# One run of all eight units in place of two of four, in the transposes' four banks, with the blocks reordered

## The chip, the cores and the metric

The kernel runs on one core of one Trainium2 chip. The metric is the device time of one execution in microseconds; lower is better. Engines are named as in the profile: PE is TensorE, DVE is VectorE, ACT is ScalarE, POOL is GpSimd, SP is SyncE, and PEld is the weight load of PE.

## What is computed

One decoder layer on 256 tokens of width 4096: a norm, one wide input projection, two groups that work on its columns, and one output projection.

```python
proj = einsum('btd,dc->btc', rms_norm(x, norm_pre_g), w_in)       # 4096 -> 14528 columns
rwkv_in, g_rwkv, glu_v, glu_g, g_conv = split(proj)
xs = rwkv_in + (prev - rwkv_in) * mu_shift                          # r, k, v and two bottlenecks
S_t = S_{t-1} diag(w_t) + (S_{t-1} (-kk_t)) (kk_t a_t)^T + v_t k_t^T # 32 heads of 64
y_t = S_t r_t
y_rwkv = (group_norm(y) * lnx_g + lnx_b + bonus) * silu(g_rwkv)
c = depthwise_conv31(glu_v * sigmoid(glu_g)) + conv_b
c = silu(layer_norm(c)) @ w_pw2 + b_pw2
y_conv = c * silu(g_conv)
out = concat(y_rwkv, y_conv) @ w_out
return x + rms_norm(out, norm_post_g)
```

## The kernel before

**The main product.** The three projections are 41 blocks of up to 512 output columns: 29 for `w_in`, 4 for `w_pw2`, 8 for `w_out`. A block is a row of slots, one for each 128 rows of its weights (32, 16 and 32). In a slot the weight tile is split into a rounded half `wh` (ACT, `w_hi`) and the rest `wl` (DVE, `w_lo`), and PE runs six matmuls, three for each half of the tokens, into `acc`. `w_hi` is issued 4 slots ahead and `w_lo` 3 (`HI_LEAD`, `LO_LEAD`).

**The side work.** What the two groups need is written as generators (`job_shift`, `job_prep`, `job_inv`, `job_chain`, `job_conv`, `job_ln`, `job_gate` and others) in lanes "0" to "5". The order on PE, DVE and ACT is written out by the program: behind each slot's matmuls `Side.step` calls the lanes in their order, one step of each, and goes on with those that yielded 0, as long as `room` holds, that is, while the summed costs of DVE and of ACT lie below those of PE. The costs are the program's own formulas (`dve_cost`, `act_cost`, `pe_cost`); a small matmul counts 45 ns, a main one of 512 columns 0.417 x 512 + 3. `CREDIT` limits how far an idle engine's sum may lag. Where the main product needs something that the side work has not issued yet (`side.drain`), the lanes run on without main matmuls.

**The recurrence.** 32 heads are 8 units of 4. For each unit `job_prep` builds records of 8 chunks of 32 tokens and stores them in `rec_dr`; for each two units `job_inv` inverts the small triangular matrices (`t_x`, loaded back as `c_x`). `job_chain` then walks through the 8 chunks for four units at a time, so it runs twice. `side_of` splits the four units of a run into two sides that use opposite rows of the array. In a chunk PE has three groups of small matmuls into `pz`, two banks wide: G12, the records' product (`qs` by `uv`) and the state's product (`ar` by `S`); G3, the inverse (`xt` by `ry`); G45, the growth of the state (`bkt` by `uv`) and the outputs (`qs` by `uv`). In G12 the units of side 1 are done in two halves of 32 columns (`HALVES`). Between the groups ACT copies `ry`, ACT and DVE copy `uv`, and DVE adds the outputs and the state. The yields between them put each at least one slot behind the last. The third and fourth `job_inv` wait for the first run's end. PSUM's eight banks are 4 for `acc`, 2 for transposes and other short products (`tp`), 2 for `pz`.

**The order of blocks.** For each group g of two units: k, r, v, then the gate and value blocks of the convolution (`gg`, `gv`); then `gc` (4), `g` (4), `w_pw2` (4), `w_out` (8). A block's eviction into one of two `pt` tiles adds its jobs. `job_conv` transposes `gv` and runs 31 taps on DVE in lane 5, the last in order. `job_ln` starts when the recurrence and the four convolutions are done, and the first block of `w_pw2` needs its result, four of its 16 rows at a time.

## Time and profile before

| | |
|---|---|
| median of 3 runs | 1817.35 us (1817.13 to 1818.72) |
| the profiled execution | 1820.06 us, span 1818.3 us |
| PE busy | 1805.0 us |
| PEld busy | 1486.4 us |
| DVE busy | 1339.7 us |
| ACT busy | 1011.6 us |
| POOL busy | 204.7 us |
| moved by DMA | 404.93 MB |

Busy time is the union of an engine's instructions. An engine's mean over the span hides stages in which it is full. A matmul's duration overlaps the next one's, so what a matmul costs PE is read from the distance of starts. An fp32 matmul that is no transpose shows as two records.

### The profile page before, as it was taken

The numbers are of one execution on the slowest core, as the hardware profiler recorded it, in microseconds if no ns is written. First come the engines' busy times: TensorE is split into PE (matmuls) and PEld (weight loads), VectorE is DVE, ScalarE is ACT, GpSimd is POOL, SyncE is SP. The second block draws the span as 40 slices with busy tenths as digits, with TensorE's granted clock in tenths as the row PEclk, the third lists the DMA queues.
The fourth block names the chain that finished last, engine by engine and source line by source line (L and its number), as shares of the span: only waits on it lengthen the run. The fifth ranks groups of instructions, "written<-read, shape, count | busy, mean of one in ns | idle before, by whom it ended". The sixth has DMA issues, their size and how long they took to land.

```text
span 1818.3 us, 30793 instructions
## 1 busy us (share of the span) xinstructions
PE 1805.0 (99%) x11152; PEld 1486.4 (82%) x11152; DVE 1339.7 (74%) x2668; ACT 1011.6 (56%) x1753; POOL 204.7 (11%) x346
## 2 busy tenths in 40 slices
PE   9999999999999999999999999999999999999997
PEld 7899888888878877788888888778888888888886
DVE  6655778997789976799998898567766655555555
ACT  6756665556645564555566544445575444554453
POOL 0000112031120302021041212010100000000000
PEclk9999999999999999999999999999999999999999
DMA  9867678777787778678677878766877666666665
GB/s 323 276 177 197 206 213 250 202 203 215 214 240 203 203 231 260 207 222 252 189 224 226 253 219 255 235 219 200 290 228 258 237 196 198 200 193 203 200 200 189
DMA packets 205144, 404.93 MB, mean 223 GB/s; under 512 B 16448, under 2 KB 33984, under 8 KB 204736
## 3 DMA queue, kind: packets, MB, share of 16 engines
q1 hardware_dynamic: 182224, 335.18, 60.7%
q0 software_dynamic: 22624, 67.66, 11.9%
q8 instruction: 87, 1.43, 0.3%
q14 instruction: 65, 0.53, 0.1%
q10 hardware_dynamic: 144, 0.13, 0.0%
HBM read 371.45 MB, written 31.46 MB: 222 GB/s over the span
## 4 chain that ended last, share of the span: by engine, by line
PE 97%; DVE 1%; DMA 1%; issue 0%; ACT 0%; POOL 0%; DVEq 0%; POOLq 0%
PE acc L92 91%; PE tp L92 3%; PE pz L92 2%; DMA c_y<-n_dr 1%; DVE chl L92 0%; DVE wl L92 0%; DVE cw L92 0%; DMA c_ar<-in_xT 0%; DVE c_y L92 0%; POOL c_y L624 0%; ACT wh L92 0%; DVE c_st L92 0%; ACT c_st L92 0%; DVE t_bk L92 0%; DVE c_s L92 0%
## 5 line engine op out<-in xcount | busy, mean ns | idle before, releaser
L92 ACT ACTIVATE wh<-wr 128x512 fp32r<-128x512 f32 (+1 forms) x1243 | 767.0, 623 | 652.6 <-PE acc L92 381.2
L92 DVE TENSOR_TENSOR wl<-wr,wh 128x512 fp32r<-128x512 f32 (+1 forms) x1243 | 830.5, 677 | 328.8 <-ACT wh L92 321.6
L92 PE MATMUL acc<-wh,lh 128*128 128x512 f32 (+1 forms) x2358 | 923.9, 392 | 1.2 <-ACT wh L92 1.2
L92 PE MATMUL acc<-wl,lh 128*128 128x512 f32 (+1 forms) x2358 | 911.8, 387 | 0.8 <-DVE wl L92 0.8
L92 PE MATMUL acc<-wh,ll 128*128 128x512 f32 (+1 forms) x2358 | 911.5, 387 | 0.0
L92 PEld LDWEIGHTS acc<-wh,lh 128*128 128x128 f32 x2358 | 443.3, 188 | 90.5 <-ACT wh L92 2.5
L92 PEld LDWEIGHTS acc<-wh,ll 128*128 128x128 f32 x2358 | 443.1, 188 | 88.6
L92 PEld LDWEIGHTS acc<-wl,lh 128*128 128x128 f32 x2358 | 443.7, 188 | 86.1 <-DVE wl L92 3.0
L92 DVE SCALAR_TENSOR_TENSOR cw<-up,pv,cw 128x256 f32<-128x256 f32 x480 | 218.0, 477 | 0.4
L92 PE MATMUL acc<-wh,chl 128*128 128x512 f32 x256 | 82.4, 397 | 0.0
L92 PEld LDWEIGHTS acc<-wh,chl 128*128 128x128 f32 x256 | 48.2, 188 | 10.9
L92 PE MATMUL acc<-wl,chl 128*128 128x512 f32 x128 | 50.5, 394 | 0.0
L533 POOL DMA_DIRECT2D rec_dr<-c_ar x16 | 14.4, 903 | 279.6 <-DVE c_ar L92 270.3
L92 ACT ACT_TABLE_LOAD x32 | 41.1, 1283 | 3.1 <-PE tp L92 1.4
L92 DVE TENSOR_SCALAR c_st<-pz 32x256 f32<-32x256 f32 x32 | 13.6, 426 | 33.8 <-ACT c_st L92 33.4
L1079 POOL DMA_DIRECT2D bb<-in_norm_post_g x8 | 4.3, 539 | 303.3 <-DVE chl L92 258.8
L649 POOL DMA_DIRECT2D c_x<-x_dr x64 | 35.1, 555 | 17.5 <-DMA x_dr<-t_x 15.3
L680 POOL DMA_DIRECT2D c_st<-rec_dr x32 | 17.1, 538 | 159.1 <-DVE c_st L92 83.9
L92 DVE TENSOR_TENSOR c_sq<-t_x,c_y 128x120 f32<-128x120 f32 (+24 forms) x124 | 31.6, 255 | 4.5 <-DMA c_y<-n_dr 4.5
L92 ACT ACTIVATE pt<-acc,rstd 128x512 f32<-128x512 f32 (+3 forms) x52 | 33.9, 656 | 0.6
L92 PEld LDWEIGHTS pz<-c_st 32*32 32x32 f32 (+2 forms) x1728 | 22.3, 116 | 13.4 <-PE acc L92 4.6
L92 DVE TENSOR_TENSOR t_x<-t_x,c_sq 128x120 f32<-128x120 f32 (+24 forms) x124 | 31.5, 254 | 0.0
(184 smaller groups left out, 945.8 us busy)
## 6 DMA issues: line engine op xcount, KB each, us to landing
wr<-in_w_in SPq DMA_DIRECT2D x430, 512.0 KB, 4.5
wr<-in_w_out SPq DMA_DIRECT2D x128, 512.0 KB, 4.6
c_st<-rec_dr POOLq DMA_DIRECT2D x32, 512.0 KB, 6.9
wr<-in_w_pw SPq DMA_DIRECT2D x32, 512.0 KB, 4.4
wr<-in_w_in SPq DMA_DIRECT2D x16, 352.0 KB, 3.3
rec_dr<-c_ar POOLq DMA_DIRECT2D x16, 256.0 KB, 5.6
rec_dr<-c_q POOLq DMA_DIRECT2D x16, 256.0 KB, 4.5
rec_dr<-c_bkt POOLq DMA_DIRECT2D x8, 512.0 KB, 5.3
```

The source lines that it names most:

```text
L92: return f(*args, **kw)
L533: nc.gpsimd.dma_start(out=rec_dr[qd, :, :, un, 0, q * 64:q * 64 + 64].rearrange("c p x -> p c x"), in_=ar[:, q * 8:q * 8 + 8, :])
L649: nc.gpsimd.dma_start(out=xt[y * CH:(y + 1) * CH, un, h * 4:h * 4 + 4], in_=x_dr[2 * pr + un, y ^ (2 * h), h * 4:h * 4 + 4].rearrange("g i ...
L680: nc.gpsimd.dma_start(out=recs[c][:, un].rearrange("p n i h x -> p (n i h x)"), in_=rec_dr[qd, c, :, un].rearrange("p n i x -> p (n i x)"))
L1079: nc.gpsimd.dma_start(out=gb, in_=a["norm_post_g"][0:1, j * BN:(j + 1) * BN].broadcast_to([P, BN]))
```

## The change

`side_of` now puts units 0 to 3 on one side and 4 to 7 on the other, and `job_chain` runs once, over all eight units. `pz` is four banks wide and is opened in the four banks that transposes use otherwise (`open_mid`, `TP` = 4 in place of 2); while it is open, `tp_wait` lets no transpose start. The first products of G12 alternate between the sides and have no halves, as G3 and the outputs do. The chain opens its own SBUF pool where the preparations' was, and three more yields stand between its steps; records come in four parts instead of two, the same number of DMAs in all. The third and fourth inversion no longer wait for the first run. The blocks go k, r, v of all groups first, with only the first convolution's among them; those of the second and third convolution follow, then three `gc` blocks, the fourth convolution's and the last `gc`. `job_conv` is split: `job_up` transposes in lane 1, the taps stay in lane 5, with 8 `up` buffers for 3. In the closing normalisation the squares of one slice overlap the subtraction of the next.

```diff
+TP = 4
...
+    mid = {}
+
+    def open_mid(name, bufs):
+        if mid:
+            mid["ctx"].close()
+        mid["ctx"] = ctx.enter_context(ExitStack())
+        mid["pool"] = mid["ctx"].enter_context(tc.tile_pool(name=name, bufs=bufs, space=PSUM))
+
+    open_mid("ps_tp", TP)
...
     def tp_wait():
-        while tpn[0] >= 2:
+        while tpn[0] >= TP or "run" in rw:
...
     def side_of(u):
-        return u // 2 % 2
+        return u // 4
...
-        while ("n", 2 * pr + 1) not in rw or (pr > 1 and not rw.get(("done", pr // 2 - 1))):
+        while ("n", 2 * pr + 1) not in rw:
...
-    def job_chain(qd):
-
-        rp = rw["pool"]
-        while ("prepd", 4 * qd + 3) not in rw or "xt" not in rw["quad", qd]:
+        rw["inv", pr] = True
+
+    def job_chain():
+
+        while any(("prepd", u) not in rw for u in range(8)) or any(("inv", pr) not in rw for pr in range(4)):
             yield "wait"
-        d = rw.pop(("quad", qd))
-        pc, xt = d["pc"], d["xt"]
-        ys = rp.tile([P, 4, 4, 2, 64], F32, name="c_y", bufs=1)
-        S = pz = ry = None
+        rw["run"] = True
+        while tpn[0] > 0:
+            yield "wait"
+        for _ in range(3):
+            yield
+        rw["ctx"].close()
+        rw["ctx"] = ExitStack()
+        rp = rw["pool"] = rw["ctx"].enter_context(tc.tile_pool(name="rc", bufs=1))
+        open_mid("ps_ch", 1)
+        pc, xt = rw["pc"], rw["xt"]
+        ys = rp.tile([P, 4, 8, 2, 64], F32, name="c_y", bufs=1)
+        S = ry = None
+
+        pz = mid["pool"].tile([P, 4, 4, P], F32, name="pz")
 
         RX, RD = slice(0, 64), slice(64, 128)
-        UN = range(4)
-        SIDES = ((0, slice(0, 2)), (1, slice(2, 4)))
-        PAIRS = (0, 2, 1, 3)
-        HALVES = ((slice(0, 64),), (slice(0, 32), slice(32, 64)))
+        UN = range(8)
+        PAIRS = (0, 4, 1, 5, 2, 6, 3, 7)
         recs = {}
 
-        def fetch(c, half):
+        def fetch(c, part):
 
             if c < NCH:
-                if half == 0:
-                    recs[c] = rp.tile([P, 4, 4, 2, 64], F32, name="c_st", bufs=2)
-                un = slice(2 * half, 2 * half + 2)
-                hold(recs[c][:, 2 * half, 0, 0, 0:1])
-                nc.gpsimd.dma_start(out=recs[c][:, un].rearrange("p n i h x -> p (n i h x)"), in_=rec_dr[qd, c, :, un].rearrange("p n i x -> p (n i x)"))
+                if part == 0:
+                    recs[c] = rp.tile([P, 8, 4, 2, 64], F32, name="c_st", bufs=2)
+                un = slice(2 * part, 2 * part + 2)
+                hold(recs[c][:, 2 * part, 0, 0, 0:1])
+                nc.gpsimd.dma_start(out=recs[c][:, un].rearrange("p n i h x -> p (n i h x)"), in_=rec_dr[c, :, un].rearrange("p n i x -> p (n i x)"))
 
         def swap(x):
             return x.rearrange("p b n x -> p n b x")
 
         def outputs(c):
-            if c % 2 == 0:
-                vec.tensor_tensor(out=ys[:, c // 2], in0=swap(pz[:, :, :, RX]), in1=ry, op=ALU.add)
-            else:
-                for sd, nn in SIDES:
-                    for rows in VR[1 - sd]:
-                        vec.tensor_tensor(out=ys[rows, c // 2, nn], in0=swap(pz[rows, :, nn, RX]), in1=ry[rows, nn], op=ALU.add)
-
-        for _ in range(8):
-            yield
-        for half in range(2):
-            fetch(0, half)
-            yield
+            for sd in range(2):
+                b = slice(2 * sd, 2 * sd + 2)
+                for rows in VR[1 - sd] if c % 2 else (slice(0, P),):
+                    vec.tensor_tensor(out=swap(ys[rows, c // 2, 4 * sd:4 * sd + 4]), in0=pz[rows, b, :, RX], in1=ry[rows, b], op=ALU.add)
+
+        for part in range(4):
+            fetch(0, part)
             yield
         for _ in range(5):
             yield
         for c in range(NCH):
-            vrs, urs = ([R[(c + n // 2) % 2] for n in UN] for R in (VR, UR))
+            vrs, urs = ([R[(c + u // 4) % 2] for u in UN] for R in (VR, UR))
             ar, qs, bkt, uv = (recs[c][:, :, i] for i in range(4))
             if c > 0:
                 outputs(c - 1)
-                Sn = rp.tile([P, 4, 2, 64], F32, name="c_s", bufs=2)
-                dec = pc[:, :, c - 1::8].unsqueeze(3).broadcast_to([P, 4, 2, 64])
+                yield
+                Sn = rp.tile([P, 16, 64], F32, name="c_s", bufs=2)
+                dec = pc.rearrange("p s q n c -> p (s q n) c")[:, :, c - 1:c].broadcast_to([P, 16, 64])
+                grown = pz[:, :, :, RD].rearrange("p b n x -> p (b n) x")
                 if S is None:
-                    vec.tensor_tensor(out=Sn, in0=swap(pz[:, :, :, RD]), in1=dec, op=ALU.mult)
+                    vec.tensor_tensor(out=Sn, in0=grown, in1=dec, op=ALU.mult)
                 else:
-                    vec.tensor_tensor(out=Sn, in0=swap(pz[:, :, :, RD]), in1=S, op=ALU.add)
+                    vec.tensor_tensor(out=Sn, in0=grown, in1=S, op=ALU.add)
                     vec.tensor_tensor(out=Sn, in0=Sn, in1=dec, op=ALU.mult)
                 S = Sn
                 yield
-                fetch(c + 1, 0)
                 yield
-                fetch(c + 1, 1)
-            else:
-                fetch(1, 0)
-            pz = ps_ch.tile([P, 2, 4, P], F32, name="pz")
-
-            for n in UN:
-
-                for o in HALVES[n // 2]:
-                    for q, h in DIAG:
-                        pe.matmul(pz[HS[q ^ h], h, n, RX][o], qs[vrs[n][q], n, h, o], uv[vrs[n][q], n, h, :], start=n == 0, stop=S is None and n == 3)
-            for n in UN if S is not None else ():
+            fetch(c + 1, 0)
+            yield
+            fetch(c + 1, 1)
+            for u in PAIRS:
                 for q, h in DIAG:
-                    pe.matmul(pz[HS[q ^ h], h, n, RX], ar[HS[h], n, q, :], S[HS[h], n, q, :], start=False, stop=n == 3)
-            if c == 0:
-                fetch(1, 1)
-            yield
-            ry = rp.tile([P, 4, 2, 64], F32, name="t_x", bufs=1)
-            act(out=ry, in_=swap(pz[:, :, :, RX]), func=AF.Copy)
-            yield
-            for n in PAIRS:
-                ur = urs[n]
+                    pe.matmul(pz[HS[q ^ h], u // 4 * 2 + h, u % 4, RX], qs[vrs[u][q], u, h, :], uv[vrs[u][q], u, h, :],
+                              start=u % 4 == 0, stop=S is None and u % 4 == 3)
+            for u in UN if S is not None else ():
                 for q, h in DIAG:
-                    pe.matmul(pz[ur[q], h, n, RX], xt[ur[q ^ h], n, h * 4 + c // 2, :], ry[ur[q ^ h], n, h, :], start=True, stop=True)
-            yield
-            for sd, nn in SIDES:
-                ur = urs[2 * sd]
-                act(out=uv[ur[0], nn], in_=swap(pz[ur[0], :, nn, RX]), func=AF.Copy, scale=-1.0)
-                vec.tensor_scalar(out=uv[ur[1], nn], in0=swap(pz[ur[1], :, nn, RX]), scalar1=-1.0, scalar2=None, op0=ALU.mult)
-            yield
-            for n in UN if c < NCH - 1 else ():
+                    pe.matmul(pz[HS[q ^ h], u // 4 * 2 + h, u % 4, RX], ar[HS[h], u, q, :], S[HS[h], u // 4 * 8 + q * 4 + u % 4, :],
+                              start=False, stop=u % 4 == 3)
+            yield
+            ry = rp.tile([P, 4, 4, 64], F32, name="t_x", bufs=1)
+            act(out=ry, in_=pz[:, :, :, RX], func=AF.Copy)
+            fetch(c + 1, 2)
+            yield
+            yield
+            for u in PAIRS:
+                ur, b = urs[u], u // 4 * 2
                 for q, h in DIAG:
-                    pe.matmul(pz[HS[h], q, n, RD], bkt[HS[q], n, h, :], uv[HS[q], n, h, :], start=True, stop=True)
-            for n in PAIRS:
-                ur, ro, k0 = urs[n], vrs[n], CH * ((c + n // 2) % 2)
+                    pe.matmul(pz[ur[q], b + h, u % 4, RX], xt[ur[q ^ h], u, h * 4 + c // 2, :], ry[ur[q ^ h], b + h, u % 4, :], start=True, stop=True)
+            yield
+            for sd in range(2):
+                ur, nn, b = urs[4 * sd], slice(4 * sd, 4 * sd + 4), slice(2 * sd, 2 * sd + 2)
+                act(out=uv[ur[0], nn], in_=swap(pz[ur[0], b, :, RX]), func=AF.Copy, scale=-1.0)
+                vec.tensor_scalar(out=uv[ur[1], nn], in0=swap(pz[ur[1], b, :, RX]), scalar1=-1.0, scalar2=None, op0=ALU.mult)
+            fetch(c + 1, 3)
+            yield
+            yield
+            for u in UN if c < NCH - 1 else ():
                 for q, h in DIAG:
-                    pe.matmul(pz[ro[q ^ h], h, n, RX], qs[ur[q], n, h, k0:k0 + CH], uv[ur[q], n, h, :], start=True, stop=True)
+                    pe.matmul(pz[HS[h], u // 4 * 2 + q, u % 4, RD], bkt[HS[q], u, h, :], uv[HS[q], u, h, :], start=True, stop=True)
+            for u in PAIRS:
+                ur, ro, k0 = urs[u], vrs[u], CH * ((c + u // 4) % 2)
+                for q, h in DIAG:
+                    pe.matmul(pz[ro[q ^ h], u // 4 * 2 + h, u % 4, RX], qs[ur[q], u, h, k0:k0 + CH], uv[ur[q], u, h, :], start=True, stop=True)
             yield
         outputs(NCH - 1)
-        bvs = rp.tile([P, 4, 512], F32, name="c_st", bufs=2)
-        for n in UN:
-            nc.gpsimd.dma_start(out=bvs[:, n], in_=bv_dr[4 * qd + n])
+        open_mid("ps_tp", TP)
+        del rw["run"]
...
+    def job_up(j, u):
+        cv["up", j] = ups = []
...
+    def job_conv(j):
+        while len(cv.get(("up", j), ())) < 4:
+            yield "wait"
+        ups = cv["up", j]
...
+            side.add("1", job_up(j, sg))
+            side.add("5", job_conv(j))
...
-    for g in range(4):
+
+    def add_krv(g):
         for kind in "kvr" if g == 0 else "krv":
             if g == 0 and kind == "r":
                 add(win, [(COL["r"], RL0)], NK, X, ev_r0)
                 add(win, [(COL["r"] + RL0, BN - RL0), (COL["low"], 2 * LORA)], NK, X, ev_low)
             else:
                 add(win, [(COL[kind] + g * BN, BN)], NK, X, ev_shift(kind, g))
+
+    def add_conv(g):
         add(win, [(COL["gg"] + g * BN, BN)], NK, X, ev_gg(g))
         add(win, [(COL["gv"] + g * BN, BN)], NK, X, ev_gv(g))
-    for j in range(4):
+
+    def add_gc(j):
         add(win, [(COL["gc"] + j * BN, BN)], NK, X, ev_gc(j))
+
+
+    add_krv(0)
+    add_conv(0)
+    for g in range(1, 4):
+        add_krv(g)
+    add_conv(1)
+    add_conv(2)
+    for j in range(3):
+        add_gc(j)
+    add_conv(3)
+    add_gc(3)
```

## Rows read from the trace of the kernel before

**Rows 1.** The page, part 1: span and busy time.

```profile
span 1818.3 us, 30793 instructions
...
PE 1805.0 (99%) x11152; PEld 1486.4 (82%) x11152; DVE 1339.7 (74%) x2668; ACT 1011.6 (56%) x1753; POOL 204.7 (11%) x346
```

**Rows 2.** Waits of PE: who for whom, total us, times, longest.

```profile
PE acc L92 <- ACT wh L92: 1.2, 2, 0.8
```

**Rows 3.** The chain that ended last: start us, us, what.

```profile
1469.24 338.91 PE acc L92 x1494
```

**Rows 4.** Timeline of PE, a chunk of the second chain run: start, us, instruction.

```profile
1173.01 0.39 PE L92 MATMUL acc<-wh,ll 128*128 128x512 f32 x1
1173.32 0.84 PE L92 MATMUL pz<-c_st 32*64 32x64 f32 x48
1174.10 0.69 PE L92 MATMUL pz<-c_s,c_st 64*64 64x64 f32 x32
1174.72 0.50 PE L92 MATMUL acc<-wh,lh 128*128 128x512 f32 x1
1175.06 0.40 PE L92 MATMUL acc<-wl,lh 128*128 128x512 f32 x1
...
1177.66 0.45 PE L92 MATMUL pz<-t_x,c_x 32*32 32x64 f32 x32
1178.05 0.50 PE L92 MATMUL acc<-wh,lh 128*128 128x512 f32 x1
```

**Rows 5.** Timeline of PE, a preparation's product of 64 records.

```profile
217.85 1.16 PE L92 MATMUL tp<-c_ar,t_bk 64*64 64x64 f32 x64
218.94 0.50 PE L92 MATMUL acc<-wh,lh 128*128 128x512 f32 x1
```

**Rows 6.** Timeline of ACT: evictions of the 15th, 19th and 24th block.

```profile
677.25 0.69 ACT L92 ACTIVATE pt<-acc,rstd 128x512 f32<-128x512 f32 x1
...
884.90 0.69 ACT L92 ACTIVATE pt<-acc,rstd 128x512 f32<-128x512 f32 x1
...
1115.24 0.69 ACT L92 ACTIVATE pt<-acc,rstd 128x512 f32<-128x512 f32 x1
```

**Rows 7.** The last preparation's product (chain of work), the second chain's first (timeline).

```profile
1001.64 1.09 PE tp L92 x64
...
1133.49 0.84 PE L92 MATMUL pz<-c_st 32*64 32x64 f32 x48
```

**Rows 8.** Convolution tile alone, by stretch: window, length, DVE busy, POOL busy, clock, DMA.

```profile
633.00:755.00 122.00, 1.45 (x5) 0.56 (x1) 1.00 0.74 235
...
998.00:1122.00 124.00, 56.63 (x126) 0.56 (x1) 1.00 0.81 234
1122.00:1240.00 118.00, 1.00 (x3) 0.55 (x1) 1.00 0.73 238
```

**Rows 9.** All engines by stretch: PE, PEld, DVE, ACT, POOL busy, clock, DMA.

```profile
1040.00:1080.00 40.00, 40.00 (x180) 33.12 (x179) 39.93 (x113) 20.39 (x34) 1.09 (x2) 1.00 0.75 220
...
1180.00:1230.00 50.00, 50.00 (x835) 38.43 (x834) 30.77 (x59) 21.25 (x39) 5.28 (x10) 1.00 0.69 221
```

**Rows 10.** Timeline of DVE: reads of PSUM in the chain and in the layer norm.

```profile
1179.51 0.43 DVE L92 TENSOR_SCALAR c_st<-pz 32x256 f32<-32x256 f32 x1 [0.44 <-ACT c_st L92]
...
1182.20 1.72 DVE L92 TENSOR_TENSOR c_y<-pz,t_x 32x256 f32<-32x256 f32 x4 [0.93 <-PE pz L92]
...
1291.33 1.21 DVE L92 TENSOR_TENSOR c_c<-c_c,tp 128x1024 f32<-128x1024 f32 x1
```

**Rows 11.** The page, part 6: the chain's records, KB each, us to landing.

```profile
c_st<-rec_dr POOLq DMA_DIRECT2D x32, 512.0 KB, 6.9
```

**Rows 12.** Tiles of the norm and second product: duration ns, first and last start us.

```profile
L92 PEld LDWEIGHTS tp<-csum,cst x4: 187/188/189, 1287.0 to 1308.1; 128*128 128x128 f32 x4
...
L92 PE MATMUL acc<-wh,chl x256: 390/393/483, 1365.9 to 1458.4; 128*128 128x512 f32 x128
L92 DVE TENSOR_TENSOR chl<-c_c,chl x4: 1217/1220/1221, 1330.5 to 1368.0; 128x1024 fp32r<-128x1024 f32 x4
```

More of the change, by code (lines that the diff above doesn't have):

```diff
@@ L252, in tp_get @@
         tpn[0] += 1
-        return ps_tp.tile(shape, F32, name="tp")
+        return mid["pool"].tile(shape, F32, name="tp")
     def tp_put():
@@ L545, in job_prep @@
         yield 0
-        vec.tensor_copy(out=pc, in_=pt_[:, :, CH])
+        vec.tensor_copy(out=rw["pc"][:, u // 4, :, u % 4, :], in_=pt_[:, :, CH].rearrange("p (q c) -> p q c", q=2))
         yield
         bq = rp.tile([P, 512], F32, name="t_0", bufs=1)
-        while tpn[0] > 0:
+        while tpn[0] > TP - 2 or "run" in rw:
             yield "wait"
@@ L756, in job_chain @@
-        for n in UN:
-            nc.gpsimd.dma_start(out=bvs[:, n], in_=bv_dr[4 * qd + n])
+        open_mid("ps_tp", TP)
+        del rw["run"]
+        bvs = rp.tile([P, 8, 512], F32, name="c_st", bufs=2)
+        for u in UN:
+            nc.gpsimd.dma_start(out=bvs[:, u], in_=bv_dr[u])
         yield 0
-        mv = rp.tile([P, 2, 32], F32, name="c_mv", bufs=1)
+        mv = rp.tile([P, 2, 64], F32, name="c_mv", bufs=1)
         mn, vr = mv[:, 0], mv[:, 1]
         y3 = ys.rearrange("p c n h x -> p (c n h) x")
-        for b in range(4):
-            sl = slice(b * 8, b * 8 + 8)
+        SL = [slice(b * 8, b * 8 + 8) for b in range(8)]
@@ L765, in job_chain @@
+        for sl in SL:
             vec.tensor_reduce(out=mn[:, sl], in_=y3[:, sl, :], axis=AX.X, op=ALU.add)
@@ L783, in job_chain @@
         vec.reciprocal(out=vr, in_=vr)
-        for b in range(4):
-            sl = slice(b * 8, b * 8 + 8)
+        for sl in SL:
             yb = y3[:, sl, :]
@@ L789, in job_chain @@
         yield
-        for n in UN:
-            u = 4 * qd + n
-            yo = bvs[:, n].rearrange("p (c t) -> p c t", t=CH)
+        for u in UN:
+            yo = bvs[:, u].rearrange("p (c t) -> p c t", t=CH)
             yield from tp_wait()
@@ L827, in job_conv @@
             yield
+    def job_conv(j):
+        while len(cv.get(("up", j), ())) < 4:
+            yield "wait"
+        ups = cv["up", j]
+        for half in range(2):
             c0 = j * 4 + half * 2
-            c = cvp.tile([P, 2, T], F32, name="cw", bufs=2)
+            c = cv["cvp"].tile([P, 2, T], F32, name="cw", bufs=2)
             for q in range(2):
                 ct = c0 + q
-                vec.tensor_scalar(out=c[:, q, :], in0=ups[q][:, 0:T], scalar1=par("conv_w", ct * CK), scalar2=par("conv_b", ct),
+                vec.tensor_scalar(out=c[:, q, :], in0=ups[2 * half + q][:, 0:T], scalar1=par("conv_w", ct * CK), scalar2=par("conv_b", ct),
                                   op0=ALU.mult, op1=ALU.add)
@@ L909, in job_gate @@
     def job_gate(j, sg):
-        yield from open_conv()
+        while "sq" not in cv:
+            yield "wait"
         cp = cv["pool"]
@@ L915, in job_gate @@
         m = cv["m"]
-        while "sq" not in cv:
-            yield "wait"
         yl = cp.tile([P, 2, 2, T], F32, name="ln_q", bufs=1)
@@ L976, in f @@
                 side.add("3", job_inv(g))
-                if g % 2:
-                    side.add("2", job_chain(g // 2))
+                if g == 3:
+                    side.add("2", job_chain())
         return f
@@ L1010, in open_conv @@
     def open_conv():
-        while not rw.get(("done", 1)):
+        while not rw.get("done"):
             yield "wait"
-        if "pool" not in cv:
-            for _ in range(5):
-                yield
-        if "pool" not in cv:
-            rw["ctx"].close()
-            cv["pool"] = ctx.enter_context(tc.tile_pool(name="cp", bufs=1))
+        for _ in range(5):
+            yield
+        for x in (rw["ctx"], rw["keep"], cv["ctx"]):
+            x.close()
+        cv["pool"] = ctx.enter_context(tc.tile_pool(name="cp", bufs=1))
     def ev_gg(j):
```

68 lines of the change are left out of this document (31 added, 37 removed).

## The prediction

> **What bounds the kernel now.** I read the head of the page first: PE is busy for 1805.0 of 1818.3 us [rows 1]. A busy PE can still be one that is fed late, so the list of PE's waits comes next: the largest entry for the main product is 1.2 us in all [rows 2]. The main product is never short of weights, so time can only be won by taking work off PE's queue, or lost by starving it. A long undisturbed piece of the chain that ended last gives the main product's price: 338.91 us for 1494 matmuls, 0.2269 us each, 1.36 us for a slot of six [rows 3]. The profiled execution took 1820.06 us for its span of 1818.3; the median of the runs is 1817.35. I make the sum as a difference within that execution and take it from the median, 2.7 us lower.
>
> **What stays.** The same blocks with their 7488 main matmuls run in another order; shifts, preparations, inversions and convolutions issue the same instructions. These go together at nothing on PE. SP's weight loads follow the blocks, none is added. What changes on PE is the chain: 16 chunks of four units become 8 chunks of eight.
>
> **A chunk before.** It has three visits to the chain's banks. The first, G12, lasts from the start of the last main matmul ahead of it (1173.01) to that of the second one behind it (1175.06): 2.05 us, less two matmuls at 0.227, is 1.60 us [rows 3, 4]. Its phases take 0.78 us (48 records: 16 of 32x64 tiles for side 0, 32 of 32x32 tiles for side 1's halves) and 0.62 us (32 records of 64x64) [rows 4]. So 0.20 us is the price of the visit itself. G3 is one phase, 32 records of 32x32: 0.39 us [rows 4], with the visit 0.59. G45 is 32 of 64x64 and 32 of 32x32: 0.62 + 0.39 + 0.20 = 1.21. The first chunk has no state product (0.98), the last no growth (0.59). Two runs: 14 x 1.60 + 2 x 0.98 + 16 x 0.59 + 14 x 1.21 + 2 x 0.59 = 22.4 + 2.0 + 9.4 + 16.9 + 1.2 = 51.9 us.
>
> **A chunk after.** 64 records of 64x64 take 1.09 us (217.85 to 218.94) [rows 5], against 0.62 for 32 [rows 4]: 0.0147 us a record and 0.15 for the phase. A 32x32 phase is then 0.15 plus 32 x 0.0075, and 64 such records take 0.63 us. The new first phase has no row: 64 records of 32x64, the two sides alternating, no halves. If the sides overlap it costs what 32x32 does, 0.63; if not, what the first 16 records do, (0.78 - 0.39 - 0.15) / 16 = 0.015 each, 1.11. I take 0.63: the sides read different rows of the array, as alternating units of G3 do. The Trainium skill, TensorEngine Tiling (Array Packing), Restrictions and Gotchas, says that different row tiles cannot reach one PSUM bank at the same time. By that rule the old order, with both sides in the same two banks, could not overlap them, and the new one with four banks can: 0.63 again, 3.8 us less over 8 chunks than by 1.11; no run here shows it. G12 becomes 0.20 + 0.63 + 1.09 = 1.92, G3 0.83, G45 1.92. One run: 7 x 1.92 + 0.83 + 8 x 0.83 + 7 x 1.92 + 0.83 = 35.2 us (39.0 with the dear first phase). **PE's queue gets shorter by 16.7 us** (12.9); 24 visits fewer at 0.20 are 4.8 of that, the rest is phase starts and the halves.
>
> **What comes to lie beside the chain.** The value block of the last group is now the 15th, and the 15th block was evicted at 677; conv2's value block is the 19th, for which 885 stands, conv3's the 24th, at 1115 [rows 6]. Before, the last group's value block was that 19th one; its second preparation's product came 117 us later, at 1002, the first chain matmul of the second run another 132 us later [rows 6, 7]. The change has five yields fewer there. Without the first chain run, 26 us of PE that lay ahead of that, the chain starts near 672 + 117 + 125 = 914 us, and conv2 is ready at 885 - 26 = 859. Conv1, 64 slots or 87 us ahead of it, needs 56.6 us of VectorE, which took 124 us when shared with an inversion [rows 8]: it ends near 900, and **conv2 runs beside the chain**. Before, the chain runs had almost no convolution beside them, 1.45 us in 633 to 755 and 1.00 in 1122 to 1240 [rows 8], and VectorE was busy for 30.8 of 50 us there; beside a convolution it is full, 39.9 of 40, with PE busy all the time [rows 9].
>
> **Why that costs.** The order written out by the planner hands side work to VectorE until its summed costs reach PE's (`room`). A small matmul counts 45 ns there (`pe_cost`), so a chunk of 160 counts 7.2 us and will take 1.92 + 0.83 + 1.92 = 4.67: 2.5 us of convolution are handed out for time that does not pass. (Before: 88 x 0.045 = 3.96 against 3.40.) Against this a main matmul counts 0.2165 us and takes 0.2269, which gives back 0.06 a slot; a chunk has 11 yields and skips some 4 slots behind its large VectorE steps, so 15 x 0.06 = 0.9 us. Reads of PSUM are dearer than planned, 0.43 us against 0.34 for 32x256 [rows 10]: 0.5 us a chunk over all. And between the sides' copies of u VectorE waited 0.44 us for ScalarE [rows 10], about 0.6 with twice the elements. Sum: 2.5 - 0.9 + 0.5 + 0.6 = 2.7 us a chunk. There are 56 us of convolution to place, and a chunk has room for 15 x (1.30 - 0.60) + 7.2 - 5.8 of its own = 11.9, so 4.7 chunks are full: 12.7 us. Low halves are issued three slots ahead (`LO_LEAD`), 4.1 us, the chain's operands two or three, so I let VectorE fall 3 us behind at no price: **PE waits about 10 us**. Bounds: 0, if the lag is absorbed or conv2 falls elsewhere, and 15, with no cushion and 3.2 us a chunk. With the dear first phase a chunk counts 0.5 less: 7.7 us of waits.
>
> **Smaller things.** Steps of 128x1024 are new in the chain; from PSUM that form takes 1.21 us on VectorE [rows 10], less than two of 512, and ScalarE, whose copy doubles too, is busy for 21.3 of 50 us beside a chain [rows 9]. The records are fetched by 32 issues of 512 KB on POOL's queue before and after, 6.9 us to landing [rows 11]; the last part of a chunk is issued some eight slots, 11 us, ahead of its use, past the gates' and conv2's writes, so it is covered, and 1 us late on each of 8 chunks would cost 8. No transpose can run while the chain holds the banks, so evicted tiles wait: two are allowed, conv2's is read before the chain starts, and the gate blocks return theirs at once. Were conv2's caught, one tile would still be free. Four transposing banks instead of two free nothing on PE, which waited for none.
>
> **The rivals.** *Forecast: a good part is lost to VectorE.* 1817.35 - 16.7 + 10 = 1810.7; net gains from 4 to 12 us belong here, and with the dear first phase 1817.35 - 12.9 + 7.7 = 1812.2. The Trainium skill, TensorEngine Tiling (Array Packing), PSUM Bottleneck, warns that tiling speeds up TensorE but not the evacuation of PSUM, which may become the limit; by that rule it comes out here too. For it speak the planner's price and that no old chain had convolution beside it. Chance 0.45.
> *PE's gain in full.* 1817.35 - 16.7 = 1800.7, if the lag is absorbed, as all full stretches are now [rows 9]. Against it: in none of those is PE's planned time above its real one. Chance 0.25.
> *No difference.* The change does not do what it says, the sides do not overlap, and VectorE gives the rest back: 1817.35 - 12.9 + 12 = 1816.5. Chance 0.16.
> *Slower: the layer norm comes late.* Conv3 is evicted near 1115 - 26 + 35 + 10 = 1134. The chain ends near 914 + 110 slots (150) + 35 + 10 = 1109; its closing normalisation is twice as long and goes first. Conv3, 124 us when shared and some 25 more, would end near 1283 and the norm's first matmul stand near 1295, 64 us ahead of the second product, which starts at 1365.9 - 16.7 + 10 = 1359. Before it was 79 us [rows 12]. The norm's last block landed at 1369 [rows 12] and was needed 12 slots into the product, at 1382: a cover of 13 us, spent by this sum to within its error. Beyond it, PE is drained and has nothing to run. 25 us late would cost some 17, since side work alone runs faster: 1810.7 + 17 = 1828. It decides from a first matmul of the norm less than 66 us ahead of the product. Against it: the plan could fill VectorE better while conv3 is awaited. Chance 0.14.
>
> **The numbers.** The predicted time is the forecast's, 1810. Forecast and full gain make faster 0.70; about 0.2%, 3.6 us, is what a measurement of this kernel can tell from no change; same 0.16, slower 0.14. The range leaves out most of the late norm and a gain above PE's own: 1799 to 1819.
>
> **What would show it.** The chain's records: 2432 instead of 2688, in 24 visits; G12 near 1.9 us, or 2.4 where the sides do not overlap. Convolution between 914 and 1050, VectorE full in the first five chunks, PE waiting there for low halves or the chain's operands, and not in the last three. Waits of PE below 3 us would make the full gain right and the cushion wrong. The norm's first matmul some 65 us ahead of the second product; a gap of PE just behind that product's start would be the drain.

## The result, and the profile after

The changed kernel takes 1809.2 us (1807.6 to 1811.0) against 1818.7 us (1817.1 to 1819.9) for the kernel before, measured beside it: a ratio of 0.9949, 95% interval 0.9935 to 0.9964, 9.5 us faster. 1810 was forecast, in a range of 1799 to 1819. The profiled execution took 1808.75 us for a span of 1806.9, which is 11.4 us less than the span of [rows 1].

The head of the page after, as in [rows 1]:

```profile
span 1806.9 us, 30142 instructions
PE 1789.4 (99%) x10896; PEld 1482.7 (82%) x10896; DVE 1341.4 (74%) x2621; ACT 1012.5 (56%) x1730; POOL 203.6 (11%) x346
```

The two entries of PE's waits in which the chain's stand, as in [rows 2] (who for whom, total us, times, longest; of the seven in the first, four lie in the chain):

```profile
PE acc L93 <- DVE wl L93: 2.6, 7, 0.5
PE pz L93 <- issue: 1.5, 3, 0.8
```

PE has 256 records fewer, the forecast 2432 against 2688 of the chain. PE's busy time fell by 15.6 us and the span by 11.4; the 4.2 between are about what the two entries hold.

PE's timeline of a chunk after, where [rows 4] shows one of before (start, us, instruction; the bracket is the idle time ahead of it and what ended it):

```profile
1017.28 0.39 PE L93 MATMUL acc<-wh,ll 128*128 128x512 f32 x1
1017.60 0.91 PE L93 MATMUL pz<-c_st 32*64 32x64 f32 x64
1018.45 1.16 PE L93 MATMUL pz<-c_s,c_st 64*64 64x64 f32 x64
1019.54 0.50 PE L93 MATMUL acc<-wh,lh 128*128 128x512 f32 x1
1019.88 0.40 PE L93 MATMUL acc<-wl,lh 128*128 128x512 f32 x1
...
1023.88 0.45 PE L93 MATMUL pz<-t_x,c_x 32*32 32x64 f32 x31
1024.58 0.46 PE L93 MATMUL pz<-t_x,c_x 32*32 32x64 f32 x33 [0.25 <-issue]
1024.97 0.50 PE L93 MATMUL acc<-wh,lh 128*128 128x512 f32 x1
...
1029.29 1.95 PE L93 MATMUL pz<-c_st 64*64 64x64 f32 x128
```

G12 takes 1019.88 - 1017.28 - 2 x 0.227 = 2.15 us; over seven chunks the mean of starts gives 2.14, the first chunk's 1.04. G3 takes 0.99 where nothing disturbs it, G45 2.08 (the last 0.99). The 24 visits sum to 1.04 + 7 x 2.14 + 8 x 0.99 + 7 x 2.08 + 0.99 = 39.5 us, against 51.9 before: **the undisturbed chain is 12.4 us shorter**, where 16.7 was forecast. The second G3 row stands in the middle of a phase: PE stopped behind record 31 of 64, and no engine or queue of the profile is named for it. Pauses of this kind in chunks 3, 4 and 5 (counted from 0) make their G3 phases 2.0 us longer.

Convolution beside the chain, the tile of the taps alone by stretch (window, length, DVE busy, POOL busy, clock, DMA), where [rows 8] had 1.45 and 1.00 us beside a whole run:

```profile
943.00:968.00 25.00, 7.86 (x19) 0.00 (x0) 1.00 0.71 228
968.00:991.40 23.40, 8.18 (x20) 0.00 (x0) 1.00 0.76 263
991.40:1017.60 26.20, 7.57 (x18) 0.55 (x1) 1.00 0.73 236
...
1136.00:1258.00 122.00, 55.75 (x126) 0.57 (x1) 1.00 0.74 213
```

Each of three chunks has 7.6 to 8.2 us of taps beside it, where the prediction had room for 11.9. Conv2 lies beside the chain (924 to 1102, forecast 914 to 1109), conv3 behind it, done at 1258 (forecast 1283).

PE's list of waits names low halves; here is DVE's timeline ahead of one of them, and PE's row at its end:

```profile
1006.22 2.79 DVE L93 TENSOR_TENSOR c_y<-pz,t_x 32x512 f32<-32x512 f32 x4
1009.03 1.30 DVE L93 TENSOR_TENSOR wl<-wr,wh 128x512 fp32r<-128x512 f32 x2
1010.36 1.23 DVE L93 TENSOR_TENSOR c_s<-pz,c_s 128x1024 f32<-128x1024 f32 x1
1011.62 1.23 DVE L93 TENSOR_TENSOR c_s<-c_s,c_pc 128x1024 f32<-128x1024 f32 x1
1012.76 1.89 DVE L93 TENSOR_TENSOR wl<-wr,wh 128x512 fp32r<-128x512 f32 x3
...
1013.50 0.50 PE L93 MATMUL acc<-wl,lh 128*128 128x512 f32 x1 [0.54 <-DVE wl L93]
```

Four output additions and two steps of 128x1024 stand in DVE's order with two low halves among them; the three that come behind are late, and the first of them holds PE. This happens three times (964, 1013, 1063), each with 0.88 to 0.93 us between two main matmuls in place of 0.227, 2.0 us together. A fourth stop that the list puts down to a low half, 0.68 us at 1093, is none (timelines of DVE and PE):

```profile
1085.38 3.09 DVE L93 TENSOR_TENSOR wl<-wr,wh 128x512 fp32r<-128x512 f32 x5
...
1092.50 0.69 DVE L93 TENSOR_TENSOR wl<-wr,wh 128x512 fp32r<-128x512 f32 x1 [0.99 <-ACT wh L93]
...
1093.20 0.39 PE L93 MATMUL acc<-wl,lh 128*128 128x512 f32 x1 [0.51 <-DVE wl L93]
```

The low half that ended just then belongs to a later slot. Counted in the order of slots, this matmul reads the fourth of the five in the first row, which ended at 1087.87, 5.3 us ahead; at 964, 1013 and 1063 the same count gives a low half that ended 0.05 to 0.06 us ahead of the matmul. The stop at 1093 is of the kind of the pauses, as the last section shows. So PE's waits for low halves in the chain are 2.0 us, where 10 was forecast. The chain as a whole gained 12.4 - 2.0 - 0.7 - 2.0 = 7.7 us, of the 9.5 between the medians; the other 1.8 is not placed.

The norm and the second product, as in [rows 12]:

```profile
L93 PEld LDWEIGHTS tp<-csum,cst x4: 188/188/189, 1272.3 to 1293.3; 128*128 128x128 f32 x4
...
L93 PE MATMUL acc<-wh,chl x256: 387/389/477, 1356.6 to 1447.3; 128*128 128x512 f32 x128
```

The norm's first matmul is 1356.6 - 1272.3 = 84 us ahead of the product (79 before, 64 forecast).

### The profile page after: what moved, and what is told of

Read it like the earlier page. It is cut to its first block, busy times and chain, and to the rows that moved or that the text cites. A ratio compares the mean times of both kernels' runs of the same rounds, so it can differ in the third digit from the quotient of the medians.

```text
span 1806.9 us, 30142 instructions
## 1 busy us (share of the span) xinstructions
PE 1789.4 (99%) x10896; PEld 1482.7 (82%) x10896; DVE 1341.4 (74%) x2621; ACT 1012.5 (56%) x1730; POOL 203.6 (11%) x346
## 3 DMA queue, kind: packets, MB, share of 16 engines
q0 software_dynamic: 22624, 67.66, 11.7%
## 4 chain that ended last, share of the span: by engine, by line
PE 93%; DVE 4%; issue 1%; DMA 1%; ACT 0%; POOL 0%; DVEq 0%; POOLq 0%
PE acc L93 88%; PE tp L93 3%; PE pz L93 2%; DVE wl L93 1%; DVE c_sq L93 1%; DVE t_x L93 0%; DMA c_y<-n_dr 0%; DVE c_y L93 0%; DVE chl L93 0%; DVE cw L93 0%; DVE c_st L93 0%; DVE c_s L93 0%; ACT c_st L93 0%; DMA c_ar<-in_xT 0%; ACT wh L93 0%
## 5 line engine op out<-in xcount | busy, mean ns | idle before, releaser
L93 ACT ACT_TABLE_LOAD x34 | 43.6, 1283 | 4.0 <-DVE t_pi L93 2.3
L645 POOL DMA_DIRECT2D x_dr<-t_x x32 | 18.3, 650 | 118.5 <-DVE t_x L93 118.5
L93 DVE RECIPROCAL t<-t 128x128 f32<-128x128 f32 x32 | 29.2, 934 | 0.3
```

The source lines that it names most:

```text
L93: return f(*args, **kw)
L645: nc.gpsimd.dma_start(out=xv[rho][:, un], in_=xi[rho * 32:(rho + 1) * 32, un])
```

## The experiments

All comparisons are with the changed kernel's 1809.2 us, each kernel measured beside the kernel before; a time without a range is one execution. The kernel before had medians of 1817.25 to 1818.72 us in these measurements, so a difference of 1 to 2 us between two kernels is not told from none.

### The cap on what is handed out: CREDIT lifted while the chain runs

```diff
-            self.base[i] = max(self.base[i], pe - m.ns - CREDIT)
+            self.base[i] = max(self.base[i], pe - m.ns - self.credit)
...
         rw["run"] = True
+        side.credit = 6000.0
...
         del rw["run"]
+        side.credit = CREDIT
```

> The changed kernel with CREDIT at 6000 instead of 1500 while the chain runs, so that the room which a group of small matmuls opens is kept for the slots behind it. Theory A (CREDIT cuts what the planner hands out: in the changed kernel a chunk got some 7.5 to 8 us of convolution, where I had reckoned 11.9): convolution rises to 11 us or more in the full chunks, VectorE is full there, and PE's waits in the chain rise from about 3 us to about 10; time 1809 + 7 = 1816. Theory B (the cap plays no part, the room is used up by something else): 7.5 to 8 us a chunk as now, time within 2 us of 1809.

Measured: 1825.0 us (1821.1 to 1827.2), ratio to before 1.0035 (1.0021 to 1.0050), 15.8 us more than the changed kernel. The tile of the taps in two chunks:

```profile
945.40:972.30 26.90, 11.70 (x28) 0.00 (x0) 1.00 0.65 209
972.30:998.70 26.40, 12.17 (x30) 0.55 (x1) 1.00 0.72 240
```

And PE's waits:

```profile
PE acc L93 <- DVE wl L93: 12.3, 10, 3.8
PE pz L93 <- issue: 4.4, 4, 1.6
```

With the cap lifted a chunk gets 11.7 and 12.2 us of taps, the 11.9 of the prediction, and PE waits 12.3 us for low halves: 8.1 in the chain, and 3.8 in one wait at 1111, just behind it, where DVE runs the last outputs and the first steps of the closing normalisation. So the forecast's mechanism exists, at about its size of 10 us; in the changed kernel the cap holds it off. The time is 9 us above the 1816 that was expected: these waits and the pauses are 12.6 us more than in the changed kernel, and the other 3 are not placed. `room` forgives an idle engine no more than 1.5 us of lag, so most of what the overpriced small matmuls of a visit would hand out is forfeited before the next slot.

### The price of a small matmul: 33 ns in place of 45

```diff
-    return max(1.69 * n, 80.0) if args[1].shape[0] == P else 45.0
+    return max(1.69 * n, 80.0) if args[1].shape[0] == P else _small[0]
...
         rw["run"] = True
+        _small[0] = 33.0
...
         del rw["run"]
+        _small[0] = 45.0
```

> The changed kernel with a small matmul counted at 33 ns in place of 45 in the written order while the chain runs: a chunk of 160 then counts 5.3 us, about what it measured with its pauses (5.2). Theory F, the forecast's: the overpriced small matmuls are what hands out too much side work; with a true price some 1.9 us a chunk less are handed out, convolution beside a chunk falls from 7.6 to 8.2 us to about 6, PE's four waits for low halves (2.8 us in all) vanish, about 3 us faster or, where the convolution then ends too late for the norm, slower. Theory C: most of the overprice is forfeited anyway, because an idle engine's sum may lag by 1.5 us only (with that limit lifted, convolution went up to 11.7 to 12.2 us a chunk): convolution per chunk falls by less than 1 us, the waits stay between 1.5 and 3 us, and the time within 2 us of 1809.

Measured: 1808.0 us (1806.8 to 1809.4), ratio 0.9946 (0.9931 to 0.9961). Two chunks of taps:

```profile
943.60:968.30 24.70, 7.12 (x17) 0.00 (x0) 1.00 0.72 234
...
991.30:1017.80 26.50, 8.35 (x20) 0.55 (x1) 1.00 0.74 239
```

And PE's waits:

```profile
PE acc L93 <- DVE wl L93: 1.4, 4, 0.5
```

With the price taken down by a quarter the taps hardly fall, 7.1 to 8.4 us a chunk. Two of the three waits behind a burst (964 and 1063) shrink from 0.5 to 0.1 us, so that the three cost 1.2 us and not 2.0, which lies between the two theories; the time cannot be told from the changed kernel's. So under the cap the price decides little, as the second theory had it. The two waits shrank where one or two taps fewer stood in the chunk (17 for 19 and 17 for 18); that this is the reason is not shown.

### DVE's burst split: one more yield between the two steps of the state

```diff
                     vec.tensor_tensor(out=Sn, in0=grown, in1=S, op=ALU.add)
+                    yield
                     vec.tensor_tensor(out=Sn, in0=Sn, in1=dec, op=ALU.mult)
```

> The changed kernel with one more yield between the two steps that make the new state (add, then multiply). Theory A (PE's waits for low halves, four of about 0.7 us in the changed kernel, come from one burst on VectorE: the outputs of an odd chunk, 2.79 us, and the two state steps, 2.4 us, with low halves queued behind): the four waits go, 2 to 3 us less, 1806.5; the chain is some 7 slots longer. Theory B (they come from VectorE lagging behind under the convolution all through): the waits stay, 1809.

Measured: 1806.7 us (1805.5 to 1807.4), ratio 0.9936 (0.9922 to 0.9949). PE's waits:

```profile
PE pz L93 <- issue: 1.3, 2, 0.8
...
PE acc L93 <- DVE wl L93: 0.2, 1, 0.2
```

The three waits behind the burst are gone, with the same 53 us of taps beside the chain. They came from the burst, not from a shortage of DVE over a whole chunk. They were 2.0 us; the medians lie 2.5 us apart, but against the kernel before, each beside its own, the gain is 10.5 us for this kernel and 9.5 for the changed one, and the two intervals overlap. That the waits go is shown, that the time falls is not. The fourth wait that the expectation counted is no wait for a low half, as said above.

### Both edits together

```diff
+        _small[0] = 33.0
...
                     vec.tensor_tensor(out=Sn, in0=grown, in1=S, op=ALU.add)
+                    yield
                     vec.tensor_tensor(out=Sn, in0=Sn, in1=dec, op=ALU.mult)
```

> The two edits that each took PE's waits for low halves away, together: one more yield between the two steps of the state's sum (alone 1806.7 against 1809.2), and a small matmul counted at 33 ns while the chain runs (alone 1808.0). Theory A, both work on the same 2.8 us of waits: no more than the yield alone, 1806 to 1807.5, waits for low halves below 0.5 us in the chain, what is left being the pauses inside the dense phases. Rival B, they add up because fewer taps also shorten what queues on DVE elsewhere: 1804 to 1806.

Measured: 1806.7 us (1806.0 to 1808.2), ratio 0.9937 (0.9923 to 0.9950): no more than the yield alone. Both work on the same waits: no wait for a low half of over 0.1 us is left in the chain. The list of PE's waits has one of 1.3 us there that it puts down to DVE (`c_st`); it stands at record 5705, a place of the series in the last section. The kernels with the yield cannot be told apart by time.

### Taps held until the fifth chunk

```diff
         rw["run"] = True
+        rw["held"] = True
...
+            if c == 4:
+                del rw["held"]
...
+                    while "held" in rw:
+                        yield "wait"
```

> The changed kernel with the convolution's taps held back from the chain's start to its fourth chunk, so that no convolution lies beside chunks 0 to 3. Lag theory (the forecast's): PE's wait for a low half in the second chunk (about 0.7 us in the changed kernel) vanishes. Burst theory: it stays near 0.7 us. The held work fits into the stretch behind the chain where VectorE has no convolution, so the layer norm is not late and the time stays within 3 us of 1809.

Measured: 1837.5 us, 28 more than the changed kernel, where the same time was expected. The wait in the second chunk (964) is gone, so the taps do take part in it. But the held taps were not made up behind the chain: they ended at 1315 and not 1259. PE's waits:

```profile
PE acc L93 <- ACT chl L93: 13.2, 4, 4.7
PE acc L93 <- DVE chl L93: 3.5, 4, 1.3
```

The norm and the second product, as in [rows 12]:

```profile
L93 PEld LDWEIGHTS tp<-csum,cst x4: 187/188/189, 1328.5 to 1349.6; 128*128 128x128 f32 x4
...
L93 PE MATMUL acc<-wh,chl x256: 387/389/797, 1360.9 to 1476.1; 128*128 128x512 f32 x128
```

The product's start by stretch, as in [rows 9]:

```profile
1350.00:1370.00 20.00, 15.15 (x64) 11.84 (x63) 12.25 (x21) 12.36 (x20) 1.06 (x2) 0.83 0.61 207
1370.00:1390.00 20.00, 14.08 (x50) 10.31 (x50) 11.61 (x18) 10.02 (x17) 2.12 (x4) 0.77 0.33 113
```

This is the prediction's slower rival, brought about: the norm's first matmul is 1360.9 - 1328.5 = 32 us ahead of the product, PE waits 16.7 us for the norm's blocks, and the product takes 115 us from its first to its last matmul of this kind and not 91. The granted clock is 0.83 and 0.77 there against 1.00 in the changed kernel, a mean between its two levels (1.2 and 2.4 GHz): behind waits of 2.0 to 4.7 us PE runs at the lower one for part of the stretch.

### The transposes of the value blocks back in lane 5

```diff
-            side.add("1", job_up(j, sg))
+            side.add("5", job_up(j, sg))
```

> The changed kernel with the transposes of the convolution's value blocks back in lane 5, the last in order, behind the taps of the convolution before (one lane name differs). Theory A, the new order of blocks needs the transposes ahead of the taps: conv1's and conv2's evicted tiles are both held while the older taps run, a third eviction has none, the side work has to run on without main matmuls, as in the experiment with the order alone (PE waits of 0.7 and 1.2 us at 807 and 810, main matmuls 0.43 us apart behind them); conv2's transposes come too late to be ahead of the chain and its taps do not lie beside it, so the norm's first matmul comes 40 to 60 us later (1310 to 1330, against a second product near 1356): 8 to 30 us slower than the changed kernel's 1809. Rival B, the lane makes no difference because taps and transposes are paced by DVE's room anyway: within 2 us of 1809, convolution beside the chain as before.

Measured: 1862.0 us, 53 more. The taps in the chain's stretch:

```profile
924.00:1103.00 179.00, 0.00 (x0) 0.00 (x0) 0.98 0.72 242
```

PE's waits:

```profile
PE tp L93 <- DVE csum L93: 18.3, 1, 18.3
```

The norm's first matmul:

```profile
L93 PEld LDWEIGHTS tp<-csum,cst x4: 188/237/333, 1356.2 to 1375.5; 128*128 128x128 f32 x4
```

All engines in a stretch behind it, as in [rows 9]:

```profile
1370.00:1390.00 20.00, 8.78 (x27) 6.82 (x28) 11.48 (x17) 11.20 (x16) 2.67 (x5) 0.50 0.30 92
```

Not one tap lies beside the chain, because conv2's transposes cannot run while it holds the banks. Both last convolutions come behind it, and the norm's first matmul stands at 1356, where the changed kernel starts the product. The direction was expected, the size was not (8 to 30 us). The forced drain near 640 and 808 did not occur here: that half of the first theory fell. With no taps there is no wait for a low half in the chain, the counterpart of the lifted cap. In 1370 to 1390, at the end of the wait of 18.3 us (which lasted until 1375.3) and behind it, the granted clock is 0.50, the lower level throughout.

Two prices now stand for the late norm, if its first matmul is set against 1356.6, where the changed kernel starts the product: 28 us at 28 us ahead (1328.5), 53 at none (1356.2). A line through them gives 0.9 us for each us, and nothing from some 60 us ahead on; the prediction had 17 / 25 = 0.68 and 66. It is an estimate from two single executions of kernels that differ in other things too.

### The new order of blocks alone, in the kernel before

```diff
-    for g in range(4):
+    def add_krv(g):
...
+    add_krv(0)
+    add_conv(0)
+    for g in range(1, 4):
+        add_krv(g)
+    add_conv(1)
+    add_conv(2)
+    for j in range(3):
+        add_gc(j)
+    add_conv(3)
+    add_gc(3)
```

> The kernel before with the new order of blocks alone: two chain runs of four units in two banks, as before. My sum put the order at nothing on PE: time as before within 2 us (1817 to 1820), chain still 52 us of PE in 48 visits. Rival: the order itself gains, by spreading VectorE's full stretches, 2 us or more. A late layer norm would show as a gap of PE behind the start of the second product, and a time above 1820.

Measured: 1823.7 us (1821.2 to 1826.9), ratio 1.0034 (1.0022 to 1.0046): 6 us slower than before, where nothing was expected. PE's timeline at the costliest place:

```profile
807.60 0.38 PE L92 MATMUL tp<-lowh,t 96*128 96x256 f32 x1 [0.70 <-ACT t L92]
...
810.39 0.73 PE L92 MATMUL tp<-cst,pt 128*128 128x128 f32 x3 [1.21 <-DVE pt L92]
810.77 0.78 PE L92 MATMUL acc<-wh,lh 128*128 128x512 f32 x1
811.34 0.63 PE L92 MATMUL acc<-wl,lh 128*128 128x512 f32 x1
811.77 0.63 PE L92 MATMUL acc<-wh,ll 128*128 128x512 f32 x1
```

From 807.6 to 810.8 no main matmul runs: the side work goes on alone, until a waiting `pt` tile is transposed. Behind the gaps the main matmuls stand 0.57 and then 0.43 us apart, where 0.227 is usual. PE's idle time here is 2.1 us and the slower matmuls cost some 1.6, together about the 3.6 us between the two profiled executions; the rest of the 6 is not placed. The order fits this kernel only together with other parts of the change. Which one frees it was not found: the lane of the transposes alone does not bring this drain back in the changed kernel. No run has the one chain run with the old order, so what the order is worth there stays open.

### Two transposing banks in place of four

```diff
-TP = 4
+TP = 2
```

> The changed kernel with two transposing banks for four outside the chain (the chain itself still opens four). The prediction said that four banks free nothing on PE, since PE waited for none before. Theory A: the same, within 2 us of the changed kernel (1809), waits of PE for transposing banks below 1 us in all. Rival B: the new order crowds transposes (the experiment with the order alone cost 6 us, though there the evicted tiles and not the banks were what ran out), and the banks are what saves it: 3 to 6 us slower, with side steps skipped around 640 and 808 us and PE waiting there.

Measured: 1809.3 us (1807.9 to 1811.4), ratio 0.9955 (0.9938 to 0.9972). The same: the four banks free nothing, as forecast.

### First products in unit order

```diff
-            for u in PAIRS:
+            for u in UN:
                 for q, h in DIAG:
                     pe.matmul(pz[HS[q ^ h], u // 4 * 2 + h, u % 4, RX], qs[vrs[u][q], u, h, :], uv[vrs[u][q], u, h, :],
```

> One line differs from the changed kernel: the 64 first products of a chunk come in unit order (side 0's 32, then side 1's 32) and no longer alternate between the sides. In the changed kernel the alternating phase took 0.84 us and the visit G12 2.14. Theory A, the sides overlap because neighbouring records use opposite rows of the array and different banks: in unit order the phase goes back to about 0.015 us a record, 1.0 to 1.1 us, G12 to about 2.35, 8 x 0.2 = 1.7 to 2 us more on PE's queue. Rival B, the order within the phase is nothing, and the gain over the old 0.015 us a record comes from somewhere else (the four banks, say): the phase stays at 0.84 within 0.03 and the time within 1 us.

Measured: 1810.9 us. PE's timeline of the first phase:

```profile
1018.48 0.39 PE L93 MATMUL acc<-wh,ll 128*128 128x512 f32 x1
1018.80 1.06 PE L93 MATMUL pz<-c_st 32*64 32x64 f32 x64
1019.79 1.16 PE L93 MATMUL pz<-c_s,c_st 64*64 64x64 f32 x64
```

The phase takes 0.99 us and not 0.84, G12 2.29 and not 2.14: 1.2 us in eight chunks. Alternating sides do overlap, but it is worth 0.15 us a phase, a third of the 0.48 between the prediction's ends (0.63 and 1.11). By single starts, nearly all of it lies in the first 32 records (0.29 us alternating, 0.42 in unit order); the second 32 take 0.41 and 0.43.

### PE's stream shifted by 32 records

```diff
+        for i in range(32):
+            nc.tensor.matmul(junk[:, 0:8], warm[:, 0:P], warm[:, 0:8], start=True, stop=True)
```

> The changed kernel with 32 more tiny matmuls at its very start, where TensorE is warmed up; nothing else differs. In the changed kernel PE pauses inside G3 behind record 51, 31 and 17 of 64 in chunks 3, 4 and 5 (1.01, 0.47 and 0.69 us, nothing that the profile shows being waited for), 384 matmul records apart. Theory A, the pause belongs to a place in PE's instruction stream (its instructions arrive in pieces of fixed size): with the stream shifted by 32 records, the pauses come 32 records earlier: behind record 19 in chunk 3, -1 (the phase's edge) in chunk 4, and record 51 + 20 - 32 = 39 in chunk 2. Rival B, it belongs to the time or to what the other engines and queues do then: the pauses stay behind records 51, 31 and 17 of chunks 3 to 5. Time within 3 us of 1809 by either.

Measured: 1808.8 us. The two longest pauses:

```profile
975.68 0.48 PE L93 MATMUL pz<-t_x,c_x 32*32 32x64 f32 x33
977.04 0.45 PE L93 MATMUL pz<-t_x,c_x 32*32 32x64 f32 x31 [0.88 <-issue]
...
999.87 0.41 PE L93 MATMUL pz<-t_x,c_x 32*32 32x64 f32 x19
1000.77 0.69 PE L93 MATMUL pz<-t_x,c_x 32*32 32x64 f32 x45 [0.49 <-issue]
```

In chunk 3 the pause moved from behind record 51 to behind record 19, 32 earlier; chunk 2 has one behind 33 (39 was expected), and chunks 4 and 5 have none left inside G3. The pause belongs to a place in PE's stream of instructions, not to a time nor to what DVE does then.

## Why the prediction was right, point by point

**The time is right, two of its terms are not.** PE's gain was put at 16.7 us and is 12.4, or 9.7 with the pauses and the stop at 1093. The loss to VectorE was put at 10 us; the waits for low halves in the chain are 2.0. Their difference was forecast as 6.7 and measured as 7.7: two errors of 7 and 8 us that nearly cancel. That the time came within 1 us of the forecast is luck; the direction and the form of the loss are not. The range left room for either error.

**The step that mis-sized PE's gain** is "a 32x32 phase is then 0.15 plus 32 x 0.0075". G3 with 64 records is a visit of 0.99 and thus a phase of 0.79, so that the second 32 records cost 0.40 us where 0.24 was assumed. A slope drawn from one length and a fixed part borrowed from another tile shape did not hold. By single starts the first 32 records of a G3 take 0.24 us from the first to the last, as the 32 of the kernel before do, and those behind them run slower; yet the 33 records behind the pause of chunk 4 took 0.39 us with the switch back to main matmuls (1024.58 to 1024.97 above), no more than a whole phase of 32 before. So it is not the records that are slow but what follows 32 of them without a stop; the reason is not shown. The new first phase, put at the same 0.63, took 0.84. Together these are 0.22 a G12 and 0.16 each for G3 and G45, 4.3 us on the chain. The prediction's own dear end, 12.9, is close to what came out, though not for its reason: the sides do overlap. The Trainium skill's rule, TensorEngine Tiling (Array Packing), Restrictions and Gotchas, that different row tiles cannot reach one PSUM bank at the same time, shows no price here. With separate banks alternation gains 0.15 us a phase; but G3 of the kernel before alternates the sides too, with both in the same two banks, and its 32 records take the same 0.24 us as the first 32 with four banks. The first products themselves were not run alternating in shared banks.

**The pauses were in no case.** [rows 2] and [rows 4] had no pause of this kind in the chain. The new phases brought them, 2.0 us and 0.7 more at 1093.

**The step that mis-sized the loss** is the chunk's "room for 15 x (1.30 - 0.60) + 7.2 - 5.8 of its own = 11.9". It let the whole 7.2 us of a chunk's small matmuls reach the taps. The description of the kernel names `CREDIT` as the limit of an idle engine's lag, but the sum left it out. The lifted cap gave 11.7 to 12.2 us of taps and 8.1 us of waits in the chain, so the mechanism (overpriced small matmuls hand out DVE time that does not pass) was right and its place in this kernel's order wrong. What remains is the two 128x1024 steps in one yield; the split showed that. The Trainium skill's warning that PSUM's evacuation may become the limit (TensorEngine Tiling (Array Packing), PSUM Bottleneck) comes out here as a matter of order: additions that read PSUM are 2.79 us of the burst, yet moving one step of it was enough.

**PE waiting for low halves** was named as the form the loss would take, and it is, three times beside conv2 and not once where the changed kernel's chain had no taps beside it. VectorE was not full there, as the prediction had it for the first five chunks: it was busy for 22.3 of 25.0 us between 943 and 968. "Not in the last three" chunks failed once: the wait at 1063 is in the sixth, since the taps, fewer in a chunk, lasted until 1079 and not 1050.

**Where the convolutions lie** held: conv2 beside the chain, its transposes ahead of it, chain from 924 to 1102. It rests on `job_up` in lane 1, which the prediction passed over in half a sentence; put back, it costs 53 us.

**The order of blocks at nothing on PE** was the right number for the whole change and the wrong reason: in the kernel before, it costs 6 us, more than half of it through a forced drain.

**The late norm** did not come: 84 us ahead, since conv3 was done 25 us before its forecast, against the 66 from which it would decide. The two experiments that made it late bear out the mechanism and roughly its price. **Records, banks, rough sizes of the state's steps**: 256 records fewer, no gain from four banks, as put.

## What to carry to other kernels

When an order is written out from a cost model, put the model's clamps into the sum and not its prices alone: here the limit on carried lag, not the price of a matmul, decided how much side work came to lie beside the chain. A burst that fits an engine's mean share can still starve the one behind it, and a yield inside it took 2.0 us of waits away. Before a wait is put down to an engine, check that the result which ended last is the one that is read. Price a longer phase from a row of its own length and shape, and before merging short bursts into long ones ask whether the instructions themselves can arrive that fast.

## What the hardware showed that was not expected

PE can run short of instructions. Part 3 of the page after has this queue:

```profile
q8 instruction: 85, 1.39, 0.3%
```

These are 85 packets; the kernel before has 87. PE's records are a weight load and a matmul each: 2 x 10896 / 256 = 85.1 and 2 x 11152 / 256 = 87.1. So a packet is 256 of PE's instructions, 128 records. In the changed kernel the three pauses in G3 stand at PE's records 6089, 6473 and 6857, 384 apart, three packets. In the ten kernels with one run of eight units, whatever was changed around them, the pauses of over 0.19 us between two records of a dense phase are 28: 26 of them at record 5321 or a multiple of 384 behind it, up to 7241, and two at 5833 and 6601, each 128 behind such a place. They took 0.2 to 2.6 us. In a dense phase of 64 a record takes 12 to 17 ns; the chain before, with phases half as long, shows none.

The trace also has the start and the end of each packet of this queue, and they fit. If packet n, counted from 0, brings PE's records from 128 (n + 1) + 73 on, then in all 28 pauses PE goes on 1.2 to 1.6 us behind the end of the packet that brings the record it goes on with. In twelve kernels with 1012 packets, no such first record starts sooner than 1.19 us behind its packet's end. In the changed kernel these packets start 124 records ahead of their first record in the median, and those of the three pauses 53, 37 and 23 ahead. So PE stood still because its next instructions had not arrived.

The stop at 1093 stands at record 7625, a place of the same series: its packet started 6 records ahead and ended 1.3 us before PE went on. Main matmuls stop for it too, and the list of waits then names whatever ended last beside it. The kernel with the split yield stops at 7625 with no engine named, and the kernel with both edits stops 1.8 us between two main matmuls at 5705. What makes some packets start so late, and why the length at one place varies so much (0.2 to 2.6 us at record 6857), stays open.
